# A hybrid retention and sliding-window layer on one core: when a list scheduler hands an operation to GpSimd

## The chip, the cores and the metric

The kernel runs on one core of one Trainium2 chip. The metric is device time in microseconds (us) of the whole program. Before the change it is 739.26 us, the median of three runs (738.84 to 740.07). The engines are named as in the profile: PE is TensorE's matmul stream and PEld its weight loads, DVE is VectorE, ACT is ScalarE, POOL is GpSimd, SP is SyncE (here it only issues transfers, shown as SPq).

## The reference

One layer in float32 over 2048 tokens of 1024 channels. All eight column groups come from one input projection. Four of them feed a chunked retention (rotary phase, per-head decay, a running state, group norm), and the other four a sliding-window softmax attention with QK norm, a bias table and sinks. Each result is multiplied by SiLU of its gate, and both go through one output projection.

```python
h = rms_norm(x, norm_w)
rq, rk, rv, rg, sq, sk, sv, sg = jnp.split(h @ w_in, offsets, axis=-1)
ro = group_norm(retention(rotary(rq), rotary(rk), rv)) * ret_norm_w * silu(rg)
so = sliding_window_attention(rms(sq), rms(sk), sv, sinks, rel_bias) * silu(sg)
return x + jnp.concatenate([ro, so], -1) @ w_out
```

## The kernel before, in words

**Four large products.** The projections are done as four matrix products one after the other: first the window group's q, k, v and half of the retention's v (two halves of 512 columns), then the retention's q, k and the other half of v (two halves of 384), then both gates (two of 512), last the output projection (two of 512). Each is a seven-multiplication block scheme over eight pairs of 128-token chunks: `weights` and `blocks` form sums and differences of blocks (`combine`, tiles `w` and `x`), and `products` adds the seven partial results from PSUM (tiles `acc`) into tiles `s`, `u`, `t`, `r`. For float32 precision every operand is split into a rounded high part and a low part (`split`): ACT writes the high part, and the low part, `raw - hi`, is one subtraction of two SBUF tensors. Three matmuls then stand for one, and the four products take 2700 of the profile's 4376 PE instructions. During the second and the third product, window attention (`window`, `attend`, `values`) and retention (`retention`) run beside them; the gates' multiplications (`gate`, tiles `go`) come around the start of the fourth.

**A planner makes the order.** No engine's order is written by hand. Every step is an `Op` with a cost, a due time and the buffers that it reads and writes; `Program.emit` (line 143) is a list scheduler that goes through a plan of its own in microseconds, picks at each step the operation that can start first, and emits it at once. `Order.put` (line 335) then holds each engine to that order. So all five engines run in order, and whatever stands in an engine's queue waits behind the instruction ahead of it.

**Costs.** An operation's `cost` is a dictionary from engine to (occupancy, latency, whether it uses the shared port). `dve(n)` (line 289) plans 0.067 + n/960 us for VectorE, `pool(n)` (line 297) 0.05 + 0.00234 n us for GpSimd with two inputs. In the plan operations with the flag for the shared port never overlap. `both(n)` (line 301) lists both engines for one operation:

```python
def both(n, more=0.0):
    occ, lat, shared = pool(n)
    return {"V": dve(n, True), "G": (occ + more, lat + more, shared)}
```

These are the operations with a choice, all of them of two SBUF tensors: the low part of a split without a scale (line 479), the sums of blocks without a scale (line 504, with 0.4 us more for GpSimd), `more` (line 662), rotary and its sums (lines 785 and 799: tiles `tcos`, `tsin`, `qk`), `qn` (line 1096), and the gate's multiplications (lines 1243 and 1253: tiles `go`, `r`, `t`). Operations that read PSUM are VectorE's or ScalarE's alone. Some small ones are GpSimd's alone: `own` (an affine select, line 1212), `va` (line 1003) and the QK norm's factors (`qk_norms`: `hs`, `rqk`, `fac`).

**The choice.** An operation with a choice lies in both queues of the plan, `avail["V"]` and `avail["G"]`, and the engine that takes it first removes it from the other. Before GpSimd may take it, lines 208 to 216 estimate when VectorE would have it done: `v` starts at VectorE's free time plus its cost, and grows by every operation of VectorE alone that is due no later and is ready by then (of the first twelve in its queue). GpSimd, which would start at `s` and take `occ`, is refused when it would end after `v`.

Buffers limit how far work runs ahead: 93 SBUF tiles of 512 columns (`CAP`, line 55) with shares for each purpose (`SHARE`, line 58), three PSUM banks for `acc` and five for the small products (`m`).

Of the kernel before, what the change touches and what calls it, by code (L numbers as in the profile page):

```python
# [75 lines left out]

CUTS = {"rows": 1, "columns": 2}
CHANGE, SOONER, LATER, SETTLED = 0.2, 5.0, 2.0, 1.0

# [27 lines left out]
class Program:  # L109
# [33 lines left out]
    def emit(self):  # L143
# [17 lines left out]
        while done < count:  # L161
            best = None
            for e, found in avail.items():
                top = None
                base = free[e]
                for due, n, o in found[:48]:
                    if top is not None and top[0] <= base + 1e-9 and not e == "T":
                        break
                    occ, lat, shared = o.cost[e]
                    s = max(base, o.ready)  # L170
                    if e == "T" and o.set:
                        s = max(base, o.ready + SETTLED)
                        if cut and CUTS.get(o.set) == cut:
                            due -= SOONER
                        elif o.set in CUTS and not cut:
                            due += LATER
                    if shared:
                        s = max(s, port)
                    need, short = {}, False
                    for b in o.new:  # L180
                        if b.ap is None:
                            need.setdefault(b.tag, []).append(b)
                    if any(due > now + AHEAD_OF.get(b.share, 1e9) for b in o.new):
                        continue
                    spare = 0
                    if e == "Q" and need:
                        if due > now + AHEAD:
                            break
                        spare = SPARE
                    for tag, bs in need.items():  # L190
                        if tag not in slots:
                            slots[tag] = [0.0] * COUNTS.get(tag, SMALL)
                        f = slots[tag]
                        if len(f) < len(bs) + (spare if tag == "k" else 0):
                            short = True
                            break
                        s = max(s, f[len(bs) - 1])
                        for share in {b.share for b in bs if b.share}:
                            many = used[share] + sum(b.share == share for b in bs)
                            if many > SHARE[share] - (spare if share in SPARED else 0):  # L200
                                short = True
                    if short:
                        continue
                    wait = 0.0
                    if e == "A" and o.set and table and o.set != table:
                        wait = 1.3
                        s += 2.0
                    if e == "G" and len(o.cost) > 1:

                        v = max(free["V"], o.ready) + o.cost["V"][0]  # L210
                        for d2, n2, o2 in avail["V"][:12]:
                            if d2 <= due and len(o2.cost) == 1 and o2.ready <= v:
                                v += o2.cost["V"][0]
                        if s + occ > v:
                            continue
                    if top is None or s < top[0] - 1e-9 or (s < top[0] + 1e-9 and due < top[1]):
                        top = (s, due, n, o, wait)
                if top is not None and (best is None or top[:3] < best[0][:3]):
                    best = top, e
# [3 lines left out]
            occ, lat, shared = o.cost[e]  # L223
# [14 lines left out]
            else:  # L238
                if wait:
                    s = s - 2.0 + wait  # L240
# [6 lines left out]
                if e == "T":  # L247
                    s = max(s - SETTLED, free_before, o.ready) if o.set else s
# [1187 lines left out]
```

## Time and profile before

| | |
|---|---|
| median of three runs | 739.26 us |
| the profiled execution's own time | 739.54 us |
| its span, first to last instruction | 737.8 us |
| TensorE's granted clock | 1.00 |
| PE busy | 725.0 us (98%) |
| PEld busy | 604.2 us (82%) |
| DVE busy | 598.4 us (81%), 1311 instructions |
| ACT busy | 437.7 us (59%) |
| POOL busy | 215.0 us (29%), 209 instructions |
| DMA queue q1 | 59.8% of 16 engines' span |

The page gives busy time, share and number of instructions of each engine, the chain of work that ended last (each instruction followed back to what released it), and groups of instructions written as line, engine, operation, out<-in, shape and count, then busy us, mean ns of one, and the idle time before them with its releasers. All instructions stand on line 353, the recording helper, so groups are told apart by tile names. The timeline lists runs of like instructions with start, length and, in brackets, the idle time before and what ended it. The table by windows gives each engine's busy time (with its number of instructions) in a stretch of the span, then the granted clock, the share of the DMA engines and GB/s. Matmul ends are modelled, so PE's busy time says where it stood still, not how fast it went.

### The profile page before, as it was taken

Reading aid. Unit: us, or ns where it says so; the run is one execution under the profiler, and the core shown is the slowest. Engines: PE = TensorE matmul, PEld = TensorE weight load, DVE = VectorE, ACT = ScalarE, POOL = GpSimd, SP = SyncE. Lnnn points to the kernel's source line nnn. Section 1 sums busy time; section 2 is a strip of 40 time slices with the busy share of each in tenths; the row PEclk is TensorE's granted clock in tenths of the full one; section 3 lists DMA queues with packets and bytes.
Section 4 is the critical chain, followed back from the end, with each engine's and each line's share of the span. In section 5 each row is a group of like instructions: output and inputs, shape, how many; then the busy total and the mean of one; then the engine's idle time right before and its main releaser. Section 6 shows DMA issues by size and latency. Waiting matters only on the chain.

```text
span 737.8 us, 13411 instructions
## 1 busy us (share of the span) xinstructions
PE 725.0 (98%) x4376; PEld 604.2 (82%) x4376; DVE 598.4 (81%) x1311; ACT 437.7 (59%) x1069; POOL 215.0 (29%) x209
## 2 busy tenths in 40 slices
PE   8999999999999999989999999999999999999998
PEld 6888888879898898978778778788877788888877
DVE  6998877867887877999978779759999998276872
ACT  6568945747686456776677676666577536331400
POOL 0200000056453321663511335112445101710330
PEclk9999999999999999999999999999999999999999
DMA  9959947864746167989654665199445431233722
GB/s 332 367 167 341 384 155 271 273 233 162 230 148 208 52 221 257 342 273 319 215 189 146 200 222 181 51 360 350 121 152 190 129 100 74 85 100 112 237 110 100
DMA packets 96838, 150.47 MB, mean 204 GB/s; under 512 B 11264, under 2 KB 35840, under 8 KB 96768
## 3 DMA queue, kind: packets, MB, share of 16 engines
q1 hardware_dynamic: 96192, 148.82, 59.8%
q8 instruction: 35, 0.57, 0.3%
q10 hardware_dynamic: 576, 0.79, 0.3%
q14 instruction: 35, 0.29, 0.1%
HBM read 107.56 MB, written 42.01 MB: 203 GB/s over the span
## 4 chain that ended last, share of the span: by engine, by line
PE 84%; DVE 7%; DMA 5%; issue 1%; ACT 1%; SPq 1%; POOL 0%; ACTq 0%; DVEq 0%; POOLq 0%
PE acc L353 69%; PE m L353 15%; DMA w<-in_w_in 2%; DVE x L353 2%; DVE t L353 2%; DVE go L353 1%; DMA x<-in_xt 1%; DMA aq_dram<-t 1%; DMA go<-ro_dram 1%; DVE lg L353 1%; DMA w<-in_w_out 1%; DVE w L353 1%; SPq L353 1%; ACT x L353 0%; DMA va<-aq_dram 0%
## 5 line engine op out<-in xcount | busy, mean ns | idle before, releaser
L353 PE MATMUL acc<-w,x 128*128 128x512 f32 (+1 forms) x2700 | 606.6, 380 | 1.6 <-DVE rg L353 0.5
L353 PEld LDWEIGHTS acc<-w,x 128*128 128x128 f32 x2700 | 488.7, 188 | 86.4 <-issue 7.3
L353 DVE TENSOR_TENSOR x<-x 128x512 fp32r<-128x512 f32 (+1 forms) x173 | 124.8, 742 | 23.2 <-ACT x L353 20.9
L353 ACT ACTIVATE x<-x 128x512 fp32r<-128x512 f32 x184 | 111.1, 624 | 10.4 <-PE acc L353 6.6
L353 POOL TENSOR_TENSOR x<-x 128x512 fp32r<-128x512 f32 x43 | 60.5, 1417 | 122.3 <-ACT x L353 63.7
L353 ACT ACTIVATE pm<-lg,nm 128x128 f32<-128x128 f32 x128 | 49.8, 391 | 34.0 <-DVE lg L353 32.4
L353 DVE TENSOR_TENSOR s<-acc,s 128x512 f32<-128x512 f32 (+1 forms) x64 | 41.6, 651 | 24.4 <-PE acc L353 24.2
L353 DVE SCALAR_TENSOR_TENSOR w<-w,nw_sb 128x512 fp32r<-128x512 f32 (+3 forms) x72 | 55.0, 784 | 6.7 <-ACT w L353 6.7
L353 ACT ACTIVATE w<-w 128x512 fp32r<-128x512 f32 (+1 forms) x72 | 40.4, 601 | 28.4 <-DMA w<-in_w_out 20.8
L353 POOL TENSOR_TENSOR w<-w 128x512 fp32r<-128x512 f32 (+3 forms) x24 | 33.4, 1402 | 70.4 <-ACT w L353 45.4
L353 DVE CUSTOM_DVE_ANT_0 lg<-m,bias,nsnk 128x192 f32<-128x192 f32 x128 | 45.2, 411 | 9.9 <-PE m L353 9.7
L353 DVE TENSOR_TENSOR w<-w 128x512 fp32r<-128x512 f32 (+3 forms) x72 | 49.1, 711 | 3.1 <-ACT w L353 2.8
L353 POOL TENSOR_SCALAR_AFFINE_SELECT own<-pT 64x512 f32<-64x512 f32 x32 | 23.0, 730 | 76.6 <-ACT pT L353 55.9
L353 ACT ACTIVATE x<-go 128x512 fp32r<-128x512 f32 x40 | 23.6, 623 | 24.9 <-PE acc L353 20.5
L353 DVE TENSOR_TENSOR t<-acc,t 128x512 f32<-128x512 f32 (+2 forms) x33 | 21.0, 636 | 18.7 <-PE acc L353 18.6
L353 POOL TENSOR_TENSOR hs<-hs,r_all 128x40 f32<-128x40 f32 (+1 forms) x2 | 1.0, 483 | 115.4 <-DVE hs L353 115.4
L353 ACT ACTIVATE s<-acc 128x512 f32<-128x512 f32 (+1 forms) x32 | 18.1, 566 | 21.5 <-PE acc L353 20.3
L353 DVE TENSOR_TENSOR r<-acc,t 128x512 f32<-128x512 f32 (+1 forms) x32 | 20.9, 652 | 12.0 <-PE acc L353 9.7
L353 ACT ACTIVATE w<-w,nw_sb 128x512 fp32r<-128x512 f32 (+3 forms) x45 | 28.8, 674 | 2.5 <-DMA w<-in_w_in 2.4
L353 DVE TENSOR_TENSOR lg<-lg 128x128 f32<-128x128 f32 x64 | 29.1, 497 | 0.0
L353 DVE TENSOR_TENSOR t<-acc,s 128x512 f32<-128x512 f32 (+1 forms) x32 | 20.8, 650 | 9.4 <-PE acc L353 9.1
L353 ACT ACTIVATE ro<-ro,nmu,rg 128x128 f32<-128x128 f32 x64 | 25.1, 480 | 3.2 <-DVE nmu L353 3.2
(144 smaller groups left out, 843.3 us busy)
## 6 DMA issues: line engine op xcount, KB each, us to landing
x<-in_xt SPq DMA_DIRECT2D x79, 256.0 KB, 4.9
x<-s_dram SPq DMA_DIRECT2D x64, 256.0 KB, 4.2
w<-in_w_in SPq DMA_DIRECT2D x38, 256.0 KB, 5.4
s_dram<-x SPq DMA_DIRECT2D x32, 256.0 KB, 5.1
xk<-in_xtok SPq DMA_DIRECT2D x32, 256.0 KB, 5.1
res<-in_xtok SPq DMA_DIRECT2D x32, 256.0 KB, 3.4
w<-in_w_out SPq DMA_DIRECT2D x20, 256.0 KB, 3.7
aq<-aq_dram SPq DMA_DIRECT2D x16, 256.0 KB, 3.8
```

The source lines that it names most:

```text
L353: return lambda *a, **k: self.order.put(op(*a, **k))
```

## The change

The refusal at the end of the estimate gets a margin. GpSimd now takes an operation with a choice only if it would end more than 3.0 us of plan time ahead of VectorE's estimated end; else the operation stays for VectorE. Nothing else in the source changes, but since the plan is made step by step, the order of every engine's later work can change with it.

```diff
+BEHIND = 3.0
...
                         v = max(free["V"], o.ready) + o.cost["V"][0]
                         for d2, n2, o2 in avail["V"][:12]:
                             if d2 <= due and len(o2.cost) == 1 and o2.ready <= v:
                                 v += o2.cost["V"][0]
-                        if s + occ > v:
+                        if s + occ + BEHIND > v:
                             continue
```

In the built program GpSimd's two-tensor operations fall from 160 to 49 and VectorE's rise from 745 to 856. Of the 49, 38 never had a choice (16 of `va`, 22 of the QK norm's factors), so 11 of 122 operations with a choice are left on GpSimd. Two small scalings of `w` move from VectorE to ScalarE.

## The prediction

> **What bounds the kernel now.** I read the page's busy times first, then the chain of waits in order of time, then the table by windows.
>
> ```profile
> span 737.8 us, 13411 instructions
> PE 725.0 (98%) x4376; PEld 604.2 (82%) x4376; DVE 598.4 (81%) x1311; ACT 437.7 (59%) x1069; POOL 215.0 (29%) x209
> ```
> ```profile
> 8.91 132.75 PE acc L353 x584
> ...
> 176.19 1.46 PE m L353 x32
> ...
> 195.57 0.81 PE m L353 x16
> ...
> 500.56 5.57 DMA x<-in_xt
> 506.19 4.64 DMA w<-in_w_in
> ...
> 584.58 102.13 PE acc L353 x451
> ...
> 709.78 24.93 PE acc L353 x120
> ```
> ```profile
> 161.00:318.00 157.00, 157.00 (x1232) 143.91 (x1233) 127.38 (x365) 106.66 (x324) 68.57 (x76) 1.00 0.63 207
> 336.00:500.00 164.00, 163.97 (x1195) 128.95 (x1194) 133.74 (x385) 111.31 (x295) 52.93 (x51) 1.00 0.63 209
> 500.00:600.00 100.00, 96.14 (x517) 78.72 (x516) 98.52 (x164) 60.13 (x111) 34.39 (x21) 1.00 0.55 182
> ```
>
> TensorE bounds it: 725.0 of 737.8 us, at a granted clock of 1.00, in three unbroken runs of products on the chain (132.75, 102.13 and 24.93 us) and in the two middle stages without idle time. All its idle time together is 12.8 us, part of it the start and the last store, so no change of the other engines can win more than that. Only between 500 and 600 us is another engine full: DVE is busy 98.52 of 100 us, and PE stands still for 3.86.
>
> The idle times of PE, from the timeline, each with what ended it in brackets:
>
> ```profile
> 160.94 0.33 PE L353 MATMUL m<-ident,kn 128*128 128x128 f32 x1 [1.17 <-DVE kn L353]
> ...
> 325.39 0.66 PE L353 MATMUL m<-v,qk 128*64 128x128 f32 x8 [2.18 <-issue]
> ...
> 515.35 1.09 PE L353 MATMUL m<-ident,go 128*128 128x128 f32 x8 [0.74 <-DVE go L353]
> ...
> 543.15 1.62 PE L353 MATMUL acc<-w,x 128*128 128x512 f32 x6 [0.45 <-DVE rg L353]
> ...
> 565.72 0.63 PE L353 MATMUL m<-ident,go 128*128 128x128 f32 x4 [0.81 <-DVE go L353]
> ...
> 567.41 0.63 PE L353 MATMUL m<-ident,go 128*128 128x128 f32 x4 [0.38 <-DVE go L353]
> ...
> 577.65 0.63 PE L353 MATMUL m<-ident,t 128*128 128x128 f32 x4 [1.08 <-DVE t L353]
> ...
> 583.95 0.63 PE L353 MATMUL m<-ident,t 128*128 128x128 f32 x4 [0.41 <-DVE t L353]
> ...
> 703.92 5.70 PE L353 MATMUL acc<-w,x 128*128 128x512 f32 x24 [0.32 <-DVE s L353]
> ```
>
> They sum to 7.54 us, and 5.36 us of it (all but the 2.18) was ended by DVE. So the question is whether DVE is late less often when GpSimd's work comes back to it.
>
> **What moves, and what it costs DVE.** By the order of the built programs 111 two-tensor operations go from GpSimd to DVE and 11 with a choice stay. DVE takes them at its pitch, not at the length that a row shows, because neighbours overlap; GpSimd's rows are longer:
>
> ```profile
> 33.65 2.49 DVE L353 TENSOR_TENSOR x<-x 128x512 f32<-128x512 f32 x4
> ```
> ```profile
> L353 POOL TENSOR_TENSOR x<-x 128x512 fp32r<-128x512 f32 x43 | 60.5, 1417 | 122.3 <-ACT x L353 63.7 <-DVE w L353 42.2 <-DVE nm L353 9.1
> ```
>
> Four in 2.49 us, less one length of 0.68 (row at 40 to 140 us below), are three steps of 0.60 us. So 111 x 0.60 = 67 us at most come onto DVE (some have 256 or 384 columns).
>
> What DVE gets back is the time that it stands blocked. The timeline shows it: while GpSimd runs, a DVE operation on two SBUF tensors does not start its work.
>
> ```profile
> 24.12 1.20 DVE L353 TENSOR_TENSOR x<-x 128x512 fp32r<-128x512 f32 x1
> ...
> 26.57 1.78 DVE L353 TENSOR_TENSOR x<-x 128x512 fp32r<-128x512 f32 x1
> ...
> 29.54 1.78 DVE L353 TENSOR_TENSOR w<-w 128x512 fp32r<-128x512 f32 x1
> ```
> ```profile
> 23.04 1.74 POOL L353 TENSOR_TENSOR w<-w 128x512 f32<-128x512 f32 x1 [21.56 <-DVE w L353]
> 26.07 1.74 POOL L353 TENSOR_TENSOR w<-w 128x512 f32<-128x512 f32 x1 [1.29 <-DVE w L353]
> ```
>
> The DVE row at 26.57 ends 0.54 us after the GpSimd one that began at 26.07, and lasts 1.78 instead of 0.68. In the first product this trade is plain: three operations return, 3 x 0.60 = 1.8 us, and 0.52 + 1.10 + 1.10 = 2.7 us of blocking go. That stage has no stall to win, so I cost it at nothing; its cover is that PE ran 132.75 us without waiting.
>
> In the full stage, 500 to 600 us, the 21 GpSimd instructions all had a choice. Groups of DVE there, and below them the same shapes from 40 to 140 us, where GpSimd was idle:
>
> ```profile
> L353 DVE TENSOR_TENSOR x<-x 128x512 fp32r<-128x512 f32 x12 | 11.0, 924 | 0.1
> ...
> L353 DVE TENSOR_TENSOR go<-go,s 128x512 f32<-128x512 f32 x6 | 5.7, 948 | 0.2
> ...
> L353 DVE SCALAR_TENSOR_TENSOR w<-w,nw_sb 128x512 fp32r<-128x512 f32 x4 | 5.0, 1254 | 0.0
> ...
> L353 DVE TENSOR_TENSOR go<-go 128x512 f32<-128x512 f32 x5 | 4.4, 900 | 0.0
> L353 DVE TENSOR_TENSOR go<-go,g 128x512 f32<-128x512 f32 x5 | 4.4, 916 | 0.3 <-DMA go<-ro_dram 0.3
> ...
> L353 DVE SCALAR_TENSOR_TENSOR rgnt<-rg 128x16 f32<-128x16 f32 x3 | 1.6, 543 | 0.0
> L353 DVE TENSOR_TENSOR rgnt<-rgnt,vsum 128x16 f32<-128x16 f32 x3 | 1.6, 541 | 0.0
> ```
> ```profile
> L353 DVE TENSOR_TENSOR x<-x 128x512 fp32r<-128x512 f32 x37 | 25.2, 683 | 5.1 <-ACT x L353 5.1
> ...
> L353 DVE SCALAR_TENSOR_TENSOR w<-w,nw_sb 128x512 fp32r<-128x512 f32 x4 | 3.0, 746 | 0.0
> ...
> L353 DVE SCALAR_TENSOR_TENSOR rxt<-rstd_all 128x16 f32<-128x16 f32 x3 | 0.5, 176 | 0.1
> ```
>
> Blocked: 12 x 0.24 + 6 x 0.27 + 4 x 0.51 + 5 x 0.22 + 5 x 0.23 + 6 x 0.37 = 11.0 us. Added: 21 x 0.60 = 12.6 us (three of a like kind stay by the new order; I count all). The load of DVE stays within 2 us; what changes is who is hit. A blocked instruction is as long as GpSimd's, however short and urgent it is: a step of 16 columns took 0.54 us on the mean where 0.18 would do, and group norm, gates and transposes queue behind it. At 160.94 this is the whole stall:
>
> ```profile
> 158.25 2.55 POOL L353 TENSOR_TENSOR qn<-aq,fac 128x512 f32<-128x512 f32 x2
> ...
> 158.81 2.07 DVE L353 SCALAR_TENSOR_TENSOR kn<-akv,fac,wqk 128x64 f32<-128x64 f32 x2
> ```
>
> In the changed order `qn` and its `kn` stand next to each other on DVE and the next `qn` comes after them, so the 1.17 us go.
>
> **The sum.** Stall at 160.94: -1.2 us, all. At 543.15, where two of the 16-column steps were blocked: -0.4 us. From 565 to 584, 2.68 us: DVE's load stays, its order gets better; I take half, between nothing and all, -1.3 us. At 703.92: half again, -0.2 us. At 515.35 and 325.39 (0.74 and 2.18 us) nothing: the row names no engine for the second, and transfers fill the chain ahead of the first (5.57 and 4.64 us); bounds 0 and -2.9. Together -3.1 us: 739.54 - 3.1 = 736.4 us for an execution like the profiled one, which was 0.28 us above the median, so 736.1.
>
> **Costed at nothing.** In the middle stages about 60 operations come to DVE, 36 us on 261.1 busy of 321; without any return that is 297, 93%, and PE's unbroken work covers it as long as DVE's backlog stays under its lead. What waits behind each moved one is DVE's next evacuation of `acc`, and behind that the next product's bank, 0.60 us a piece. PE's own order changes too: 11 more interruptions of the products by transposes and the like. A split logits group costs 2 x 0.81 - 1.46 = 0.16 us, so 22 more changes are 3.5 us at most, and a gain of about 1 where groups join; I take 0, since a group of four transposes fits into a product's pipeline. SP's queue gets another order with the same transfers; 0, bounds 1 us either way, since the two long waits for data above cost PE only 0.74.
>
> **Rivals.**
> (1) No change: the stalls are made by transfers and by PE's order and only move. For it: both DMA pieces on the chain at 500 to 511 us. Against: DVE ended eight of the nine stalls, and no transfer ended one by its row. It gives -1.2 (the `kn` stall alone) to +1: about 738.5 us.
> (2) Slower: DVE becomes the bound between 500 and 600 us. If the blocked time is not returned, because what was blocked would have waited for data anyway, 12.6 us come onto an engine with 1.5 us to spare, so it decides from the third moved operation on. Price up to 11 us; with half of the 11.0 returned, 12.6 - 5.5 - 1.5 = 5.6 us: 745 us. For it: DVE's 98.52. Against: blocked rows there begin right behind their neighbour, with idle times of 0.0 to 0.3 us.
> The Trainium skill, Perfetto Trace Analysis, section Optimizing Scalar/DVE Operations, says that a saturated DVE may be helped by giving work to ScalarE or even GPSIMD, and adds that DVE and GPSIMD share a read port, so that it might not help. By its first half the change costs this rival's 751 at the worst; by its second the forecast holds, and the 1.78 us rows side with the second.
> (3) A larger gain: DVE's stalls and half of the 2.18 us vanish, and some of the merging: 739.3 - 5.4 - 1.1 - 1 = 732 us.
> (4) The change doesn't act: out, since 111 instructions do change engines.
>
> **Chances.** Forecast (-2 to -5 us) 0.48, larger gain 0.10, no change 0.17, slower 0.25. Within 0.2% (1.5 us, about what a measurement can tell from no change) is rival 1 alone: 0.17; faster 0.58; slower 0.25. The likeliest case alone reaches from 734.2 to 737.5. The range goes from 732 up to 744, which leaves out some 6% below and 12% above.
>
> **What would show it.** Right: POOL busy near 60 us; DVE busy within 15 us of 598.4; no 128x16 or `kn` row over 0.6 us in the timeline except beside `own` and `va`; DVE `lo` operations at 0.68; PE's idle time below 10 us, with none at `kn`. Wrong: new idle times of PE ended by DVE `x`, `s` or `t` in the stages from 161 to 500 us (rival 2 in another place), or DMA names at those of 500 to 585 us.

## The result, and the profile after

| | before | changed |
|---|---|---|
| median, runs taken together | 739.35 us (6 runs, 737.39 to 740.72) | 733.51 us (6 runs, 732.71 to 736.52) |
| ratio, 95% interval | | 0.9928 [0.9905, 0.9950] |
| profiled execution | 739.54 us, span 737.8 | 734.61 us, span 732.9 |

The change gains 5.8 us by the medians; the forecast was 3.1. These lines of the changed kernel's page answer to those of before: the span, busy times, the shares of the chain of waits, and DVE's largest group (the low parts, `x<-x`). The last two were these before:

```profile
PE 84%; DVE 7%; DMA 5%; issue 1%; ACT 1%; SPq 1%; POOL 0%; ACTq 0%; DVEq 0%; POOLq 0%
...
L353 DVE TENSOR_TENSOR x<-x 128x512 fp32r<-128x512 f32 (+1 forms) x173 | 124.8, 742 | 23.2 <-ACT x L353 20.9
```

And in the changed kernel:

```profile
span 732.9 us, 13277 instructions
PE 725.3 (99%) x4376; PEld 606.4 (83%) x4376; DVE 604.7 (83%) x1420; ACT 438.9 (60%) x1071; POOL 68.2 (9%) x98
...
PE 92%; DMA 3%; DVE 2%; SPq 1%; issue 1%; ACT 0%; ACTq 0%; DVEq 0%
...
L355 DVE TENSOR_TENSOR x<-x 128x512 fp32r<-128x512 f32 (+1 forms) x214 | 145.2, 698 | 19.9 <-ACT x L355 17.4
```

DVE runs 109 instructions more and is busy only 6.3 us longer. The `x<-x` group takes 698 ns on the mean (742 before). In the chain DVE's share falls from 7% to 2%. GpSimd keeps 68.2 of 215.0 us. PE's work is the same (725.3 against 725.0 us), and the 4.9 us that leave the span were its idle time: 12.8 us before, 732.9 - 725.3 = 7.6 after.

The table by windows of the changed kernel (start and end, length, then busy time with number of instructions of PE, PEld, DVE, ACT and POOL, the granted clock, DMA share and GB/s):

```profile
161.00:318.00 157.00, 156.59 (x1228) 143.09 (x1227) 132.19 (x398) 107.50 (x326) 33.68 (x47) 1.00 0.64 208
318.00:336.00 18.00, 17.23 (x148) 13.38 (x147) 15.62 (x32) 10.06 (x20) 3.10 (x4) 0.91 0.89 290
336.00:500.00 164.00, 163.75 (x1193) 129.16 (x1193) 136.43 (x428) 112.77 (x308) 19.97 (x21) 1.00 0.63 205
500.00:600.00 100.00, 100.00 (x547) 83.83 (x544) 98.00 (x186) 64.55 (x119) 3.88 (x3) 1.00 0.57 192
686.00:712.00 26.00, 26.00 (x116) 21.53 (x115) 20.96 (x35) 7.93 (x15) 0.00 (x0) 1.00 0.48 171
```

From 500 to 600 us DVE is as full as before (98.00 against 98.52) with 22 instructions more, and PE, which stood still for 3.86 us there, does not stand still at all. The groups of DVE in that stretch whose lengths showed the blocking before:

```profile
L355 DVE TENSOR_TENSOR x<-x 128x512 fp32r<-128x512 f32 x19 | 12.7, 688 | 0.0
...
L355 DVE TENSOR_TENSOR go<-go,s 128x512 f32<-128x512 f32 x8 | 5.7, 707 | 0.2 <-ACT s L355 0.2
...
L355 DVE SCALAR_TENSOR_TENSOR w<-w,nw_sb 128x512 fp32r<-128x512 f32 x4 | 3.0, 754 | 0.0
...
L355 DVE TENSOR_TENSOR rgnt<-rgnt,vsum 128x16 f32<-128x16 f32 x3 | 0.5, 169 | 0.0
...
L355 DVE SCALAR_TENSOR_TENSOR rgnt<-rg 128x16 f32<-128x16 f32 x3 | 0.5, 168 | 0.0
```

924 ns have become 688, 1254 have become 754, and the 16-column steps take 168 and 169 ns instead of 543 and 541.

**Where the time went.** Idle times miss a part of a stall, because ends of matmuls are modelled. Counting from the start of one PE instruction to the start of the next has no such gap. The following is added up from all PE rows of both profiled executions, between the starts of chosen product matmuls (of 2700, 672 to a product, but the last 12 are issued as 24 of half width); each stretch holds the same number of other matmuls in both. Idle time ahead of an instruction counts with the instruction before it.

```
us, from the start of product matmul to product matmul          before  changed
span start to 1008th                                             244.2    243.6
1008th to 1680th (half of 2nd, half of 3rd product: middle)      222.1    224.5
  of it  m<-v,qk                                                   9.5      6.8
         m<-qkT and m<-state,qkT                                  11.6     15.4
         acc                                                     143.9    145.0
1680th to 2016th (second half of the 3rd product, the gates)     113.2    108.1
  of it  acc                                                      83.2     80.7
         m<-ident,go                                               8.5      6.3
2016th to 2520th (4th product)                                   115.8    115.2
2520th to the last                                                39.1     38.1
```

The gain lies late: 268.1 us (the last three stretches together) become 261.4 from the 1680th product matmul to the last. The middle loses 2.4 us again. A second profile of each kernel (the repeats of experiments 7 to 9) has 268.1 and 261.3 us late and 222.5 and 224.3 in the middle. Two of the changed kernel's remaining idle times stand near the end of the second product:

```profile
327.59 0.48 PE L355 MATMUL m<-state,qkT 64*128 64x128 f32 x2 [0.38 <-DVE state L355]
328.39 0.86 PE L355 MATMUL m<-state,qkT 64*128 64x128 f32 x6 [0.32 <-DVE state L355]
```

### The profile page after: what moved, and what is told of

It reads as the page before. It is cut to its first block, busy times and chain, and to the rows that moved or that the text cites. A ratio compares the mean times of both kernels' runs of the same rounds, so it can differ in the third digit from the quotient of the medians.

```text
span 732.9 us, 13277 instructions
## 1 busy us (share of the span) xinstructions
PE 725.3 (99%) x4376; PEld 606.4 (83%) x4376; DVE 604.7 (83%) x1420; ACT 438.9 (60%) x1071; POOL 68.2 (9%) x98
## 4 chain that ended last, share of the span: by engine, by line
PE 92%; DMA 3%; DVE 2%; SPq 1%; issue 1%; ACT 0%; ACTq 0%; DVEq 0%
PE acc L355 76%; PE m L355 16%; DMA w<-in_w_in 2%; SPq L355 1%; DVE w L355 1%; DMA x<-in_xt 1%; DVE lg L355 0%; DVE x L355 0%; DVE state L355 0%; ACT x L355 0%; DVE qk L355 0%; ACT pm L355 0%; ACTq L355 0%; ACT w L355 0%; DVE st L355 0%
## 5 line engine op out<-in xcount | busy, mean ns | idle before, releaser
L355 DVE TENSOR_TENSOR x<-x 128x512 fp32r<-128x512 f32 (+1 forms) x214 | 145.2, 698 | 19.9 <-ACT x L355 17.4
L355 DVE TENSOR_TENSOR w<-w 128x512 fp32r<-128x512 f32 (+3 forms) x90 | 59.0, 681 | 0.5 <-ACT w L355 0.3
L355 DVE SCALAR_TENSOR_TENSOR w<-w,nw_sb 128x512 fp32r<-128x512 f32 (+3 forms) x72 | 52.3, 738 | 7.9 <-ACT w L355 7.7
L355 POOL TENSOR_SCALAR_AFFINE_SELECT own<-pT 64x512 f32<-64x512 f32 x32 | 24.5, 773 | 157.9 <-ACT pT L355 130.7
L355 DVE TENSOR_TENSOR x<-go,x 128x512 fp32r<-128x512 f32 x39 | 26.5, 685 | 0.0
L355 PE MATMUL m<-ks,qT 64*64 64x192 f32 x512 | 25.7, 330 | 0.0
L355 ACT ACTIVATION_READ_ACCUMULATOR pm<-lg,nm 128x1 f32 x128 | 24.3, 190 | 0.0
L355 ACT ACTIVATE c<-acc 128x512 f32<-128x512 f32 (+1 forms) x24 | 13.3, 558 | 17.5 <-PE acc L355 17.4
```

The source lines that it names most:

```text
L355: return lambda *a, **k: self.order.put(op(*a, **k))
```

## The experiments

All variants are compared with runs of the kernel before on the same chip; "late part" is the time from the 1680th product matmul to the last, "middle" that from the 1008th to the 1680th, both counted in the trace like above (before: 268.1 and 222.1; changed: 261.4 and 224.5).

**1 and 2: engine against order.** The change does two things: it puts operations on another engine, and the planner arrives at another order. The first variant keeps the order of before and issues each operation with a choice, at its place, on the engine that the changed kernel gives it:

```diff
-            o.go(engines[e])
+            o.go(engines[("G" if o.n in ON_G else "V") if "G" in o.cost and len(o.cost) > 1 else e])
```

`ON_G` holds the numbers of the 11 operations that the changed kernel has on GpSimd. Only nine of them are among the 122 that GpSimd had before; the other two are sums of `w` that were DVE's. So the 111 of the change are 113 that leave GpSimd less two that come to it.

> The plan of before, with its order of every operation, but the 111 operations that the change takes from GpSimd are issued on DVE at their place in that order. Blocking theory (the gain comes from DVE no longer standing still while GpSimd runs): the stall at kn (1.17 us) and most of the 3.9 us of PE's idle time from 500 to 600 us go, so -3 to -5.5 us against before, 734 to 736.5 us. Rival, new order (the gain comes from the different order of PE and the transfers that the changed plan makes): PE's order is the old one, so it stays within 1 us of before, or becomes slower, because DVE now holds work for which the plan gave it no time: 739 to 742 us.

Measured: 739.32 us, ratio 0.9996 [0.9978, 1.0013]. The total is what the rival expected. The late part fell to 263.8 us, as blocking would have it, but the middle rose to 227.4. The largest new stall of PE there, in its timeline, and what DVE did until then:

```profile
360.03 0.66 PE L358 MATMUL m<-v,qk 128*64 128x128 f32 x8 [2.50 <-issue]
```
```profile
353.82 5.43 DVE L358 SCALAR_TENSOR_TENSOR w<-w,nw_sb 128x512 f32<-128x512 f32 x5
359.17 0.40 DVE L358 CUSTOM_DVE_ANT_0 lg<-m,bias,nsnk 128x192 f32<-128x192 f32 x1
```

PE's row names no engine, but DVE shows who is late: the window logits (`lg`), which empty PSUM banks of the small products, stand behind 5.43 us of `w` and go on as PE does. GpSimd's rows in that stretch, and below them DVE's `w` at the same place in the kernel before, show why these five take so long:

```profile
350.48 2.27 POOL L358 TENSOR_TENSOR w<-w 128x512 f32<-128x512 f32 x1 [11.12 <-DVE w L358]
353.38 1.67 POOL L358 TENSOR_TENSOR w<-w 128x512 f32<-128x512 f32 x1 [0.63 <-DVE w L358]
357.00 1.71 POOL L358 TENSOR_TENSOR w<-w 128x512 f32<-128x512 f32 x1 [1.95 <-DVE w L358]
```
```profile
352.15 2.73 DVE L353 SCALAR_TENSOR_TENSOR w<-w,nw_sb 128x512 f32<-128x512 f32 x4
```

Three of the 11 operations on GpSimd, one of them new there, run beside DVE's `w`; the kernel before had GpSimd idle from 345.45 to 355.97 us. `lg` starts 3.1 us later than in the kernel before (359.17 against 356.07). Until the first of the three, DVE was 0.6 us behind; the rest came beside them, and the five `w` end at 359.25 us, 0.54 after the last of the three, the same distance as in the prediction's example. So the largest part of this stall is blocking once more, by what stayed on GpSimd, and not the load of what came to DVE. Right behind the stall, from 361.26 us, TensorE's granted clock is 0.50 for 3.41 us (see the last section). At half the clock that window costs up to 1.7 us, an estimate, so with the idle times of 2.50 and 0.62 us at this place it makes up most of the 5.3 us. Eleven of the twelve executions of this variant had a mean clock of 0.995 to 0.998; the one at 1.00 took 736.70 us.

The second variant is the reverse: the order of the changed kernel, with the 122 operations that GpSimd had before issued on GpSimd again (same line, `ON_G` with those 122).

> The changed plan's order, but the 122 operations that ran on GpSimd before are issued on GpSimd again. Blocking theory: GpSimd is busy about 215 us again, DVE rows are lengthened again, and the time goes back to that of before or above it, since the plan left GpSimd no time: 738 to 745 us. Rival, new order: stays near the changed kernel, 733 to 735 us.

Measured: 742.27 us, ratio 1.0028 [1.0015, 1.0042]. This total lies where blocking was expected to put it, but the loss lies elsewhere. The middle rose to 230.6 us, with 2.83 us of idle time ahead of `m<-v,qk` at 327 us. The late part was 262.9 us, near that of the changed kernel, although GpSimd works there; the stretch from 500 to 600 us in its table by windows:

```profile
500.00:600.00 100.00, 99.92 (x561) 82.87 (x560) 94.89 (x167) 67.56 (x128) 31.58 (x22) 1.00 0.60 206
```

So the two parts of the change overlap in the late stage: DVE alone brings 4.3 of 6.7 us there, the new order alone 5.2, both together 6.7. In the middle either half without the other costs 5.3 to 8.5 us, in both profiles with one window at half the clock in it.

**3 and 4: early against late.** The margin holds for late operations only (due in the last third of the third product or in the fourth), or for all others only:

```diff
-                        if s + occ + BEHIND > v:
+                        if s + occ + (BEHIND if o.due >= 150 else 0.0) > v:
```

The fourth has `o.due < 150` in its place.

> The margin of 3 us only for operations due from 150 on (the last part of the third product, the gates, the fourth product): 44 operations leave GpSimd, 78 stay. Blocking theory: PE's idle time from 500 to 600 us and around 703 us goes (3.9 + 0.5 us), the kn stall at 160.9 stays: -3.5 to -4.5 us against before, about 735 us. If the gain came from all stages alike: 44 of 111, about -2.3 us.

> The margin of 3 us only for operations due before 150: 66 operations leave GpSimd, 56 stay. Blocking theory: the kn stall (1.17 us) goes and the stalls from 500 to 600 us stay: -1 to -2 us against before, about 738 us. If the gain came from all stages alike: 66 of 111, about -3.5 us.

Measured: late only, where 44 operations leave GpSimd, 733.01 us, 0.9904 [0.9885, 0.9922]; early only, where 66 leave, 739.25 us, 0.9988 [0.9973, 1.0003]. The stretch from 500 to 600 us of each, from the tables by windows, late only first:

```profile
500.00:600.00 100.00, 100.00 (x543) 83.91 (x542) 98.36 (x188) 63.53 (x117) 1.29 (x1) 1.00 0.55 186
```
```profile
500.00:600.00 100.00, 97.83 (x528) 80.15 (x525) 97.28 (x166) 61.39 (x113) 36.22 (x24) 1.00 0.58 191
```

The 44 late operations bring the whole gain, the 66 early ones none. The middle of "late only" took 224.0 us, 1.9 more than in the kernel before, although DVE's and GpSimd's rows come in the same order in both up to about 495 us. So a single profile can't tell a difference of this size in the middle from what one order varies by.

"Late only" also tests the explanation of the stall at `kn`, since its order there is that of before. GpSimd's `qn` pair and DVE's `kn` pair are as long as before (2.55 and 2.07 us), and PE does not wait:

```profile
156.82 2.56 POOL L355 TENSOR_TENSOR qn<-aq,fac 128x512 f32<-128x512 f32 x2
```
```profile
157.39 2.07 DVE L355 SCALAR_TENSOR_TENSOR kn<-akv,fac,wqk 128x64 f32<-128x64 f32 x2
```
```profile
159.58 0.27 PE L355 MATMUL m<-ident,kn 128*128 128x128 f32 x1
```

What differs is the start of the chain: GpSimd's row of `va` ahead of them, first in the kernel before, then in "late only", then in the changed kernel:

```profile
154.53 0.73 POOL L353 TENSOR_TENSOR va<-va,vn 64x256 f32<-64x256 f32 x1 [3.95 <-DMA va<-aq_dram]
```
```profile
152.87 0.73 POOL L355 TENSOR_TENSOR va<-va,vn 64x256 f32<-64x256 f32 x1 [2.33 <-DMA va<-aq_dram]
```
```profile
155.37 0.74 POOL L355 TENSOR_TENSOR va<-va,vn 64x256 f32<-64x256 f32 x1 [4.39 <-DMA va<-aq_dram]
```

Its transfer came 1.7 us earlier in "late only", which hides the blocking, and 0.8 us later in the changed kernel, where PE does not wait for `kn` all the same, since `qn` no longer blocks it.

**5 and 6: blocking by itself.** The changed kernel, with work on GpSimd whose results nobody reads, at 43 late places. Each time a subtraction of one column (so that it starts when the operation's operand is there), then two additions of 256 columns, or five fills of 256 columns, on a tile of its own:

```diff
+            if o.n in AT_THESE:
...
+                engines["G"].tensor_tensor(PROBE[0][:, 0:1], gate, gate, ALU.subtract)
+                for _ in range(2):
+                    engines["G"].tensor_tensor(PROBE[0], PROBE[0], PROBE[0], ALU.add)
```
```diff
+                for _ in range(5):
+                    engines["G"].memset(PROBE[0], 0.0)
```

> The changed kernel; at the place of 43 of the operations that left GpSimd from the gates on, GpSimd gets work that nobody waits for: a 128x1 operation that holds it until the operation's input is there, then two adds of 128x256 that read and write SBUF (about 0.85 us each by the rows of that size). Blocking theory: DVE rows from 500 to 600 us and 686 to 710 us are lengthened again and PE's stalls there come back: +3 to +7 us against the changed kernel, 736.5 to 740 us. Rival, late results (the gain came because results that GpSimd delivered after 1.4 us now come after 0.6): nobody waits for this work, so within 1 us of the changed kernel, 733 to 734.5 us.

> As d1_idle_adds, but in place of the two adds five fills of 128x256 that only write SBUF (about 0.3 us each, so GpSimd is busy about as long). If DVE is blocked by GpSimd's reading, as the rows of two-tensor operations suggest: no lengthened DVE rows, within 1 us of the changed kernel. If any work on GpSimd blocks DVE: like d1_idle_adds, 736.5 to 740 us.

Measured: additions 739.84 us, 1.0005 [0.9985, 1.0024], the late gain gone (267.5 us); fills 733.85 us, 0.9923 [0.9893, 0.9954], late part 261.4 us as without them. The stretch from 500 to 600 us and three groups in it, additions first, then fills:

```profile
500.00:600.00 100.00, 95.69 (x516) 78.03 (x515) 99.79 (x173) 61.61 (x114) 51.42 (x63) 1.00 0.53 181
```
```profile
L369 POOL TENSOR_TENSOR probe<-probe 128x256 f32<-128x256 f32 x40 | 34.8, 870 | 3.1
...
L369 DVE TENSOR_TENSOR go<-m,go 128x512 f32<-128x512 f32 x16 | 10.7, 681 | 0.0
...
L369 DVE TENSOR_TENSOR t<-t,rden 128x512 f32<-128x512 f32 x8 | 7.5, 937 | 0.2 <-ACT t L369 0.2
...
L369 DVE TENSOR_TENSOR rgnt<-rgnt,vsum 128x16 f32<-128x16 f32 x3 | 1.7, 583 | 0.0
```
```profile
500.00:600.00 100.00, 100.00 (x550) 83.85 (x547) 97.80 (x186) 64.78 (x119) 46.76 (x123) 1.00 0.56 193
```
```profile
L369 POOL MEMSET probe<- 128x256 f32 x100 | 31.2, 312 | 5.8
...
L369 DVE TENSOR_TENSOR t<-t,rden 128x512 f32<-128x512 f32 x8 | 5.5, 682 | 0.0
...
L369 DVE TENSOR_TENSOR rgnt<-rgnt,vsum 128x16 f32<-128x16 f32 x3 | 0.5, 171 | 0.0
```

34.8 us of reading additions stretch the groups shown of DVE's operations on two SBUF tensors (682 to 937 ns, 171 to 583), and PE stands still for 100 - 95.69 = 4.31 us. 31.2 us of fills stretch nothing. An operation with one operand in PSUM, `go<-m,go`, keeps 681 ns beside the additions. DVE's own work is the same in both, so the 6 us between them are the price of the reads. This shows what blocking does to an order with no time for it. How much of the loss of before it was, the first variant shows: with nearly all of GpSimd's work gone from that stretch (3.91 us busy from 500 to 600 us) and the order kept, 4.3 of 6.7 us came back.

The rival, late results, is out: the additions restored the loss although nobody waits for them. In the profile of before, too, the list of waits from 466 us to the end names GpSimd as the releaser of no other engine.

**7 to 9: other margins.** `BEHIND = 1e9`, so that GpSimd takes none of these operations; and a margin of 3.0 for the late ones with 1.0 for the early:

```diff
-BEHIND = 3.0
+BEHIND = 1e9
```
```diff
-                        if s + occ + BEHIND > v:
+                        if s + occ + (BEHIND if o.due >= 150 else 1.0) > v:
```

> GpSimd never takes an operation with a choice (margin without end): the last 11 go to DVE too. Blocking theory for the late part: as the changed kernel there. In the middle stages 8 more operations come to DVE where it had no room: 733 to 736 us, the loss between 300 and 400 us.

> Margin 3 us for operations due from 150 on, 1 us for those due before: 39 operations stay on GpSimd, nearly all in the middle stages (the changed kernel 11, e3_late_only 78). If the middle stages lose in proportion to what DVE has to take there: between e3_late_only and the changed kernel, 733 to 733.5 us, with the third product's start 0 to 2 us later than in e3_late_only. If they don't depend on it: the same as e3_late_only.

Measured: none on GpSimd 731.01 us, 0.9881 [0.9847, 0.9914], better than was expected; 1.0 for the early ones 734.44 us, 0.9937 [0.9914, 0.9960], above the 733 to 733.5 that were expected. Its profile has a middle of 223.8 us and a late part of 261.3, like "late only". Five of its eleven executions had a mean clock of 1.00 and took 732.74 to 734.22 us; the other six, at 0.995 or 0.998, took 734.44 to 737.43. So the excess goes with the clock, and no dependence on the number of early operations is shown. The margin of none was run once more, beside the changed kernel and the kernel before:

> The changed kernel once more, beside the next three on the same chip. If the late part (from the 1680th product matmul on) is set by DVE's blocking alone: 261.4 us again, as in its first profile and in e3_late_only; the part before it moves by 1 to 2 us from execution to execution with the transfers. 733 to 734.5 us.

> e5_never once more beside the changed kernel. If the margin's last 11 operations cost something: 1.5 to 3 us below the changed kernel, about 731 us. If e5_never was only a lucky execution: within 1 us of it.

> The kernel before once more, for a second profile: its stall at kn near 160 us should be gone if it was the late transfer of va in that one execution that made it (e3_late_only has the same order there, and had none), and there again if GpSimd's two qn alone made it. The stalls from 500 to 600 us stay in either case. 739 to 740 us.

Measured: changed 733.22 us, 0.9911 [0.9889, 0.9933], with a late part of 261.3 us; none 730.89 us, 0.9883 [0.9863, 0.9903]; before as its own variant 738.52 us, 0.9990 [0.9973, 1.0007]. "None" was the fastest both times, 2.3 us below the changed kernel beside it. The intervals overlap, but the executions with a mean clock of 1.00 don't: 730.17 to 731.39 us (eight of "none") against 732.05 to 733.71 (eight of the changed kernel). By the starts of matmuls, the changed kernel takes 485.6 us in this profile from the 1008th product matmul to the last and "none" 482.4 us. Of these 3.2 us, 2.8 are the retention's `m<-qkT` and `m<-state,qkT` in the middle: 15.5 us against 12.7. The changed kernel's timeline prints five idle times of 0.2 us or more at them, 0.45, 0.38, 0.32, 0.21 and 0.22 us, four of them ended by DVE's `state` and `nm`; the timeline of "none" has a single one of that size between 161 us and the end:

```profile
324.89 1.08 PE L355 MATMUL m<-qkT 64*128 64x128 f32 x7 [0.56 <-ACT so L355]
```

DVE has the larger load in "none", not the smaller one (140.29 us busy from 336 to 500 us against 137.43, and 16.54 against 15.62 from 318 to 336). So it is not DVE's load; which moved operation makes `state` and `nm` late in the changed order was not tried.

The repeated kernel before has its stalls from 500 to 600 us again (PE busy 96.46 us). It shows the stall at `kn` with half its size, 0.52 us, after a `va` transfer that ended 0.4 us earlier:

```profile
160.30 0.33 PE L353 MATMUL m<-ident,kn 128*128 128x128 f32 x1 [0.52 <-DVE kn L353]
```

**10: the subtractions of `va` as well.** "None", and the 16 subtractions of `va`, which had no choice, on DVE:

```diff
-                {"G": pool(256)}, lambda e, r=r, whole=whole: e.tensor_tensor(d()[r, :], d()[r, :], whole()[r, :], ALU.subtract),
+                {"V": dve(256, True)}, lambda e, r=r, whole=whole: e.tensor_tensor(d()[r, :], d()[r, :], whole()[r, :], ALU.subtract),
```

> e5_never, and the 16 subtractions of va (64x256, two SBUF tensors, about 0.85 us each on GpSimd) go to DVE too, so that GpSimd keeps only own and the QK norm's factors. Blocking theory: 13.7 us less reading on GpSimd, 5.3 us more on DVE in stages where DVE is about 82% busy: 0 to 1.5 us faster than e5_never, 729.5 to 731 us. Rival, DVE is full there: slower than e5_never.

Measured: 731.92 us, 0.9896 [0.9877, 0.9915], 1.0 us above "none" beside it, within the intervals. No gain is left there.

## Why the prediction was right, point by point

The direction held, and so did the mechanism for the late part. 733.5 us lies inside the range (732 to 744), but 0.7 us below that of the likeliest case (734.2 to 737.5): one term of the sum was too small, and two that were put at nothing were not nothing. That the total came as near as it did is in part luck. In the two profiles the late part gave 6.7 us where 1.9 were forecast, the part up to the 1008th product matmul 0.6 where 1.2 were, and the middle took 2.4 where nothing was.

- **PE bounds, and only its idle time can be won.** Right: 12.8 us of idle time became 7.6, with PE's busy time unchanged.
- **111 operations cost DVE 0.60 us each, at most 67 us, and the blocked time comes back.** Right: DVE's busy time rose by 6.3 us only. In the full stretch 12.6 us were to come and 11.0 to return; DVE's load stayed within 0.5 us (98.52 and 98.00), and the groups fell to the lengths that they have without GpSimd.
- **565 to 584 us half of 2.68, 543 us 0.4, 703 us half of 0.32, 515 us nothing: 1.9 us in all.** This is the mis-sized term: the late part returned 6.7 us. All of these stalls went, the one at 515 us with them, which had been put down to the transfers ahead of it; its releaser in brackets, DVE `go`, was the better witness. Besides, the printed idle times understate a stall. Between the 1680th and the 2016th product matmul they add to 0.74 + 0.45 + 0.81 + 0.38 + 1.08 = 3.46 us, and 5.1 us came back there.
- **"DVE's load stays, its order gets better."** Right. The additions and fills show that blocking alone can cost the whole late gain. The new order with the old engines shows that blocking in another order costs little: PE was busy 99.92 of 100 us from 500 to 600, with GpSimd at 31.58 and DVE at 94.89. Which steps have to stand clear of GpSimd for that was not separated.
- **The stall at `kn`, -1.2 us, all of it, blamed on `qn`.** It went, and `qn` was the cause that the change takes away. But the stall needed a late `va` transfer too: with the same blocking PE waited 1.17, 0.52 or 0 us as that came later or earlier. So the term is 0 to 1.2 us from execution to execution, not 1.2.
- **The 2.18 us at 325 us costed at nothing, since its row names no engine.** Wrong: `m<-v,qk` fell from 9.5 to 6.8 us. The timeline of before shows why, first GpSimd, then DVE:

```profile
320.87 1.32 POOL L353 TENSOR_TENSOR x<-x 128x512 fp32r<-128x512 f32 x1
322.16 1.71 POOL L353 TENSOR_TENSOR tcos<-a,rp 128x512 f32<-128x512 f32 x1
```
```profile
320.99 1.76 DVE L353 SCALAR_TENSOR_TENSOR w<-w,nw_sb 128x512 fp32r<-128x512 f32 x1
322.67 1.48 DVE L353 TENSOR_TENSOR qk<-tsin,tcos 128x256 f32<-128x256 f32 x1
324.07 0.54 DVE L353 TENSOR_TENSOR t<-acc,t 128x384 f32<-128x384 f32 x1
324.54 0.40 DVE L353 CUSTOM_DVE_ANT_0 lg<-m,bias,nsnk 128x192 f32<-128x192 f32 x1
```

  Two operations (0.75 and 0.42 us where GpSimd is idle) end 0.56 and 0.28 us after GpSimd's `x` and `tcos` and take 2.1 us too long, and the logits that free the banks stand behind them. It is the same blocking, two steps further up. In "late only", where these operations stay on GpSimd, PE still waits 1.28 us at this place.
- **The middle stages costed at nothing, because PE's work covers DVE's load.** Wrong by 2.4 us net in these two profiles, and by 2.2 between the two that have no window at half the clock there (222.1 before, 224.3 in the changed kernel's second). The 2.7 us above were won and 3.8 us lost at `m<-qkT` and `m<-state,qkT` (15.5 us again in the changed kernel's second profile), 1.1 us in `acc`, of which 0.6 is left in the second profile. So PE's changed order, also put at nothing, can have cost 0.6 us in `acc`. Against a firm loss stands "late only", whose middle took 224.0 us in the order of before. DVE's load is not the reason for the loss, since "none" puts more on DVE and is faster there. The order is left as a cause that was argued and not shown, and which step of it was not settled.
- **Rivals.** No change (738.5 us) is out, and so is DVE as the bound from 500 to 600 us (745 us): the blocked time was returned. The largest stall of the first variant looks like it (DVE full, `lg` late), but is blocked time beside GpSimd's `w`. The larger gain (732 us) described the size better than the forecast did, and its terms too: DVE's stalls go and part of the 2.18 us. The Trainium skill, Perfetto Trace Analysis, section Optimizing Scalar/DVE Operations, was cited with two halves. The trace agrees with the second, the shared read port; of the shares tried on GpSimd (122 of these operations, 78, 56, 39, 11 and none), none is the fastest.
- **What was to show it.** POOL near 60 us: 68.2. DVE within 15 us of 598.4: 604.7. `lo` at 0.68: 688 ns from 500 to 600 us. Idle time below 10 us and none at `kn`: 7.6, none. No 128x16 row is over 0.6 us; of the `kn` rows one is that does not stand beside `own` or `va`, 1.02 us at 190.1 us, beside one of the two sums of `w` that came to GpSimd. The opposite signs did not appear as they were named (DVE's `x`, `s` or `t`, or DMA); the new idle times of 0.38, 0.32 and 0.22 us are ended by DVE's `state` and `nm`.

## What to carry to other kernels

Before work is given to a helper engine, compare its length there with the main engine's pitch, and look in the trace whether the main engine's short instructions become as long as the helper's: here 1.4 us of GpSimd bought 0.60 us of DVE and made a 0.17 us step take 0.54. A stall whose row names no engine is followed back along the instructions that free its buffers, and printed idle times of PE can understate what may be won (3.46 us printed, 5.1 won). When operations change engine, what stays behind counts as well: the new engines in the old order won 4.3 us late and lost 5.3 in the middle, most of it where three operations left on GpSimd met DVE's. The order made for the new engines lost 2.4 there.

## What the runs showed of the hardware

GpSimd's fills (312 ns for 256 columns) lengthen none of the DVE groups shown. Its additions (870 ns) hold up those of two SBUF tensors, down to 16 columns (171 to 583 ns), but not `go<-m,go` with an operand in PSUM (681 ns). The Trainium skill, SBUF — State Buffer, section Who interferes with whom, says just this: DVE with two SBUF inputs contends with a GpSimd instruction that reads SBUF and not with one that only writes.

TensorE's granted clock fell to 0.50 for 3.41 us, from 328.76 us on, in the profiled execution of the changed kernel, without a long pause of PE before it. This is its table by windows, and the matmuls that were hit, from the timeline:

```profile
324.00:328.00 4.00, 3.54 (x26) 2.55 (x22) 2.39 (x6) 2.88 (x6) 0.00 (x0) 1.00 1.03 355
328.00:332.00 4.00, 3.68 (x19) 2.98 (x20) 4.00 (x9) 1.97 (x4) 0.00 (x0) 0.59 0.94 304
332.00:336.00 4.00, 4.00 (x52) 3.42 (x51) 3.74 (x11) 1.97 (x5) 0.32 (x1) 0.98 0.87 284
```
```profile
329.18 2.29 PE L355 MATMUL acc<-w,x 128*128 128x384 f32 x6
```

A window fitted to the fall has the clock of it alone:

```profile
328.76:332.17 3.41, 3.41 (x17) 2.75 (x16) 3.41 (x7) 1.86 (x3) 0.00 (x0) 0.50 0.93 299
```

The same six in the repeated run of the changed kernel:

```profile
327.77 1.32 PE L355 MATMUL acc<-w,x 128*128 128x384 f32 x6
```

They take 2.29 us at a clock of 0.59 and 1.32 in the repeated run, whose clock is 1.00 in that window and whose span is 731.6 instead of 732.9 us. The Trainium skill, TensorE: Matmul & The Clock Gate, section What's actually happening, states half rate after an idle window of some 3.4 us. The length and the half agree with this trace; the idle window does not, since the pauses before this dip are 0.38 and 0.32 us. The repeated run had 1.15 us of them and no dip, and in the second variant PE was busy only 1.72 of 3.41 us from 325.59 us on and the clock stayed at 1.00. What sets it off stays open.

Six of the fourteen profiled executions have such a stretch of one or two windows, between 324 and 370 us. It also goes with much of the scatter: of the changed kernel's twelve executions the eight with a mean clock of 1.00 took 732.05 to 733.71 us, the three at 0.998 733.98 to 734.72, and the one at 0.995 736.52.
